# Hybrid pooling and mLSTM block: the values projected by rows of time, and the first keys made in place

## The chip, the cores and the metric

The kernel runs on one core of a Trainium2 chip. A core has a matrix engine (TensorE, PE), whose weight loads are listed apart (PEld), a vector engine (VectorE, DVE), a scalar engine (ScalarE, ACT), a general engine (GpSimd, POOL) and a queue engine for transfers (SyncE, SP). Each takes its own instructions in order and waits for the others by semaphores. The metric is the time of one execution on the device in microseconds (us). Lower is better.

## The reference

One block over 2048 steps of 1024 channels, batch 1, float32:

```python
h = rms_norm(x, norm_pre_g)
proj = h @ w_in                        # 1024 x 9232
u_a, z_a, q, k, v, o, z_b, gates, g_a, g_b = split(proj)
pooled = window means of u_a (2, 4, 8, 16) minus u_a
y_a = (pooled @ pool_mix_w, by group) * pool_scale * silu(z_a)
q, k = split(silu(centred_depthwise_conv([q, k], 5 taps)))
# 4 heads of 256; forward and backward, in chunks of 128 steps
c_chunk = einsum('bhcld,bhcle->bhcde', kw, vc)    # kw = weighted keys
C_t = keep * C_(t-1) + add * c_chunk
num = ((q k^T) * d) v + inter_scale * (q C);  h = num / max(|den|, exp(-m))
y_b = rms_norm(h_fwd + h_bwd) * mlstm_norm_g * sigmoid(o) * silu(z_b)
merged = sigmoid(g_a + b0) * (y_a @ w_proj_pool) + sigmoid(g_b + b1) * (y_b @ w_proj_mlstm)
out = x + rms_norm(merged @ w_out, norm_post_g)
```

## The kernel before

All products keep float32 accuracy by three matmuls on split operands: an upper part (made mostly on ACT, line 98) and a lower part, which is the rest (a subtraction on POOL or DVE, line 102). `mm3` does upper by upper, upper by lower and lower by upper for four tiles of 128 rows of the contraction, which are twelve matmuls into one bank (lines 110 to 112). In names, `...h` and `...l` are upper and lower.

**Phase 1, the projection (0 to 1492 us).** Time is cut into two halves of 1024 steps, each half into two blocks of 512. The columns of `w_in` are taken in 36 pairs of two blocks of 128 columns, in the order of `in_pairs()`. For each pair and half the product is done by Strassen's scheme in `strassen`: seven products of twelve matmuls of 512 columns, into the banks A, B and C (two buffers each) instead of eight. Weights stand still in the array, x moves, and the result has channels on the partitions and time along the row. The combinations of x (`S1` to `S4`, made in `combos`) are made once a half; those of the weights (`T1` to `T4`) are made in `prep_w` in the first half, kept in memory by `keep_w`, and read back in the second by `again_w`. The first two pairs, of which the weights arrive while x is still prepared, go through `quarters` (eight products, lines 500 to 502). Beside them run the matmuls of the gates (`gps`, copied out as `gsb` on line 671) and small products that fold the pooling weights (`fps`, line 373); all three take turns in two buffers named `tr`. `busy` matmuls at the very start only keep the array at work. The loop of `phase1` interleaves a pair with the rest of the one before it: A and the S2 product of the new pair, then A22 by T4 and S4 by B22 of the old, then the new pair's S1, S3 and A12 products. `FOLDS` and `ROWS` say behind which pair other work is given out.

The values are needed with time on the partitions. So `pair_v` collects the transposed result of one head as rows `raw` (line 685) and turns it by 32 transposes (128 x 128 each, `vtr`, line 744) a head and half, splits it again (`vnh` on ACT, `vnl` on DVE) and stores it.

**Phase 2, the mLSTM (1492 to about 1830 us).** For head 0 a first backward pass comes ahead: for each chunk of 128 steps the stored `kT` is turned back by two transposes (`kt`, line 1311), copied by ACT as `kn`, weighted and split into keys (`keys`), multiplied with the values into `cu` (lines 1040 to 1042, 2 x 3 matmuls of 258 columns), and added to the state `cb` on DVE (line 1256). Later heads do the same beside other work. For that first pass `keys` has a path of its own: ACT scales to float32 (`kw`, line 1267), DVE casts (line 1268) and POOL subtracts (line 1269), in tiles of the pool `w1`, of which there are eight. All other keys go through `weigh`: ACT scales straight to the upper part (line 1244), DVE makes the lower in one pass (line 1245), in two buffers (`KB = 2`).

**After it** (to 2342 us) come the two branch projections (`paps`, and `pb` with 256 columns to a matmul), the merge and the output projection.

The order on each engine is that in which the program is written, moved by priorities and by `issue_after`, which ties an instruction behind another.

Of the kernel before, what the change touches and what calls it, by code (L numbers as in the profile page):

```python
# [38 lines left out]
PRE = 12  # L39
FOLDS = (2, 5, 7, 9, 12, 14, 16, 18)  # L40
ROWS = (3, 4, 6, 7, 9)
# [10 lines left out]
def in_pairs():  # L52

    base = dict(u=0, z=1024, q=2048, k=3072, v=4096, o=5120, zb=6144, ga=7184, gb=8208)
    one = {}
    for h in range(NH):
        for kind in ("q", "k", "v", "u", "z", "ga", "gb"):
            c = base[kind] + h * DH
            one[kind, h] = (kind, h, c, c + P)
    for j in range(8):  # L60
# [21 lines left out]
class Kernel:  # L82
# [122 lines left out]

    def combos(self, H, j, a11, a12, a21, a22):

# [13 lines left out]
    def operands(self, half, H, hp, wc, pool, psum):  # L221
# [4 lines left out]
        room = {}  # L226
        for b, q, where in ((0, 0, "raw"), (0, 2, "acc"), (0, 1, "acc"), (0, 3, "acc"), (1, 0, "raw"), (1, 2, "raw"), (1, 1, wc), (1, 3, wc)):
# [20 lines left out]
        def sums():  # L248
# [8 lines left out]
            for i in range(4):  # L257
                nc.tensor.matmul(ps[:, i : i + 1], acc[:, i * P : (i + 1) * P], self.one_c, start=True, stop=True)
# [40 lines left out]
        for b in range(2):  # L299
# [22 lines left out]
            yield  # L322
        ends = [self.combos(H, j, X[j][0], X[4 + j][0], X[j][1], X[4 + j][1]) for j in range(4)]
        yield
# [186 lines left out]
    def phase1(self):  # L511
        tc, nc, a = self.tc, self.nc, self.a
        with ExitStack() as es:
# [25 lines left out]
            for half in range(2):  # L539
# [53 lines left out]
                for i in range(2, n):  # L593
# [25 lines left out]


                    this, self.read_banks = work(i, W), []
                    next(this)
# [35 lines left out]
    def gates(self, half, H, W, psum, pool):  # L658
        nc = self.nc
        for b in range(2):  # L660
# [9 lines left out]
            g = pool.tile([32, BLK], F32, tag="p", name=self.nm("gsb"))  # L670
            nc.scalar.activation(g, ps, AF.Copy)
            t0 = half * HALF + b * BLK
# [58 lines left out]

    def pair_v(self, half, kind, h, H, W, psum, pool):
        nc = self.nc
        t = yield from self.collect(H, W, psum, pool, HALF, 0)
        for b in range(2):
            hi, lo = (pool.tile([P, 4, DH + 2], F32R, tag="acc", name=self.nm(f"vn{p}")) for p in "hl")
            nc.vector.memset(hi[:, :, DH:].bitcast(F32), 1.0)
            nc.vector.memset(lo[:, :, DH:].bitcast(F32), 0.0)
            for c2 in range(2):
                ps = psum.tile([P, 2, DH], F32, tag="tr", name=self.nm("vtr"), bufs=2)  # L740
                for c in range(2):
                    for i in range(2):
                        tt = (b * 4 + c2 * 2 + c) * P
                        nc.tensor.transpose(ps[:, c, i * P : (i + 1) * P], t[i][:, tt : tt + P], self.ident)
                cc = slice(c2 * 2, c2 * 2 + 2)
                self.split(hi[:, cc, :DH], lo[:, cc, :DH], ps, "act", "dve")
            c0 = half * 8 + b * 4
            for p, o in (("h", hi), ("l", lo)):
                nc.sync.dma_start(self.sp[f"v{p}{h}"][:, c0 : c0 + 4, :], o.bitcast(F32))

# [471 lines left out]
    def mlstm(self, turns, ends):  # L1222
        nc, tc, sp, col = self.nc, self.tc, self.sp, self.cols
        E = DH + 2
        with ExitStack() as es:
# [16 lines left out]
            def weigh(out, k, w):  # L1242

                nc.scalar.activation(out[0], k, AF.Copy, scale=w)
                nc.vector.scalar_tensor_tensor(
                    out[1], k, w, out[0].bitcast(F32), op0=ALU.mult, op1=ALU.subtract
                )

            def update(new, kw, v, old, keep):
# [10 lines left out]
            def keys(h, c, d):  # L1260

                if d == 1 and h == 0:

                    kw = self.w1.tile([P, 2, 512], F32, tag="w", name=self.nm("kw"))[:, 0, :DH]
                    k = self.w1.tile([P, 2, 512], F32R, tag="w", name=self.nm("k"))
                    out = k[:, 0, :DH], k[:, 1, :DH]
                    up = nc.scalar.activation(kw, kn[h, c // 4][:, c % 4, :], AF.Copy, scale=col["w"][:, ix(d, h, c)])
                    nc.vector.tensor_copy(out[0], kw)
                    nc.gpsimd.tensor_tensor(out[1], kw, out[0].bitcast(F32), op=ALU.subtract)
                    if c == NC_ // 2:  # L1270

                        none = last.tile([P, 1], F32, tag="none", name="none", bufs=1)
                        with tc.issue_after(up.ins):
                            nc.scalar.activation(none, self.one_c, AF.Exp)
                    return out
# [387 lines left out]
    def tail(self):  # L1663

        tc = self.tc
        with ExitStack() as es:
            w1 = self.w1 = es.enter_context(tc.tile_pool(name="w1", bufs=8, side="right", reuse_waits="tile"))
            self.kv = es.enter_context(tc.tile_pool(name="kv", bufs=KV, reuse_waits="tile"))
# [46 lines left out]
def layouts(i):  # L1715
# [3 lines left out]
    wk = w_in.reshape(KT, P, -1).transpose(1, 0, 2)  # L1719
    pair = [np.stack([wk[:, :, c : c + P].reshape(P, 2, 4, P) for c in cc], axis=2) for _, _, *cc in in_pairs()]  # L1720
    x = np.asarray(i["x"])[0]
# [42 lines left out]
```

## Time and profile before

| | |
|---|---|
| runs | 2341.11, 2343.8, 2347.96 us; median 2343.8 |
| profiled execution | 2344.1 us, its span 2342.3 us |
| granted TensorE clock, mean | 0.993 |
| matmuls | 11545 |
| transfers | 564.43 MB, mean 241 GB/s |

The times of the profile are counted from the start of the span. A row of the time line gives start, duration, engine, line, operation, result and operands; in brackets is how long the engine was idle before, and what ended it. A matmul's duration overlaps that of the next.

### The profile page before, as it was taken

The numbers are of one execution on the slowest core, as the hardware profiler recorded it, in microseconds if no ns is written. First come the engines' busy times: TensorE is split into PE (matmuls) and PEld (weight loads), VectorE is DVE, ScalarE is ACT, GpSimd is POOL, SyncE is SP. The second block draws the span as 40 slices with busy tenths as digits, with TensorE's granted clock in tenths as the row PEclk, the third lists the DMA queues.
The fourth block names the chain that finished last, engine by engine and source line by source line (L and its number), as shares of the span: only waits on it lengthen the run. The fifth ranks groups of instructions, "written<-read, shape, count | busy, mean of one in ns | idle before, by whom it ended". The sixth has DMA issues, their size and how long they took to land. (4 is left out here: it accounts for less than half of the span.)

```text
span 2342.3 us, 32965 instructions
## 1 busy us (share of the span) xinstructions
PE 2285.9 (98%) x11545; PEld 1938.1 (83%) x11545; DVE 1412.6 (60%) x2379; ACT 885.8 (38%) x1796; POOL 1184.2 (51%) x917
## 2 busy tenths in 40 slices
PE   7899999999999999999999999899999999999998
PEld 5788888888888788888878788699998888999886
DVE  6665656768765555546656565388887453454365
ACT  5334333333343423323333233467766221111342
POOL 4755545666664533356564555245556341233574
PEclk9999999999999999999999999899999999999999
DMA  5567766766685366788888787767767696677863
GB/s 211 188 237 271 259 222 223 265 234 219 222 296 206 110 203 212 228 297 279 295 298 287 265 299 270 258 193 246 238 190 243 219 321 227 214 277 256 329 207 126
DMA packets 233270, 564.43 MB, mean 241 GB/s; under 512 B 23568, under 2 KB 70800, under 8 KB 233104
## 3 DMA queue, kind: packets, MB, share of 16 engines
q1 hardware_dynamic: 233104, 562.33, 69.7%
q8 instruction: 91, 1.49, 0.3%
q14 instruction: 75, 0.61, 0.1%
HBM read 340.46 MB, written 221.77 MB: 240 GB/s over the span
## 5 line engine op out<-in xcount | busy, mean ns | idle before, releaser
L102 POOL TENSOR_TENSOR wB<-wraw,wB 128x512 fp32r<-128x512 f32 x220 | 333.1, 1518 | 293.3 <-ACT wB L98 232.7
L98 ACT ACTIVATE wB<-wraw 128x512 fp32r<-128x512 f32 x224 | 139.3, 626 | 268.7 <-PE bankB L112 121.9
L102 POOL TENSOR_TENSOR wT<-wt,wT 128x512 fp32r<-128x512 f32 x102 | 148.5, 1459 | 128.2 <-ACT wT L98 105.5
L718 DVE SCALAR_TENSOR_TENSOR acc<-raw,conv_w,acc 128x1026 f32<-128x1026 f32 (+1 forms) x96 | 151.2, 1587 | 10.5 <-ACT acc L713 9.7
L1040 PE MATMUL pb<-oxs,w_proj_mlstm 128*128 128x256 f32 x512 | 143.9, 281 | 0.7 <-DVE sga L1206 0.4
L1042 PE MATMUL pb<-oxs,w_proj_mlstm 128*128 128x256 f32 x512 | 143.9, 281 | 0.0
L1041 PE MATMUL pb<-oxs,w_proj_mlstm 128*128 128x256 f32 x512 | 143.8, 281 | 0.0
L98 ACT ACTIVATE wT<-wt 128x512 fp32r<-128x512 f32 x136 | 85.3, 629 | 153.5 <-PE bankB L112 60.4
L1385 POOL TENSOR_TENSOR qs<-q,isc 128x256 f32<-128x256 f32 x120 | 90.0, 754 | 93.1 <-PE num L1401 59.9
L110 PE MATMUL bankB<-S3h,wT 128*128 128x512 f32 x272 | 106.2, 390 | 3.6 <-DVE u L469 3.6
L110 PE MATMUL bankB<-A22h,wT 128*128 128x512 f32 x272 | 106.1, 390 | 2.1 <-DVE u L474 2.1
L110 PE MATMUL bankA<-A12h,wB 128*128 128x512 f32 x272 | 108.0, 397 | 0.0
L110 PE MATMUL bankC<-S4h,wB 128*128 128x512 f32 x272 | 106.2, 391 | 1.2 <-DVE raw L685 1.2
L112 PE MATMUL bankA<-A11h,wB 128*128 128x512 f32 x272 | 106.0, 390 | 1.3 <-POOL wB L102 1.3
L1025 POOL TENSOR_TENSOR nm<-nm,mask 128x256 f32<-128x256 f32 x64 | 60.4, 955 | 91.4 <-DMA nm<-negM 74.2
L111 PE MATMUL bankB<-S2l,wT 128*128 128x512 f32 x272 | 106.5, 392 | 0.0
L110 PE MATMUL bankC<-S1h,wT 128*128 128x512 f32 x272 | 106.4, 391 | 0.0
L111 PE MATMUL bankC<-S4l,wB 128*128 128x512 f32 x272 | 106.4, 391 | 0.0
L112 PE MATMUL bankA<-A12h,wB 128*128 128x512 f32 x272 | 106.2, 391 | 0.0
L110 PE MATMUL bankA<-A11h,wB 128*128 128x512 f32 x272 | 106.2, 390 | 0.0
L111 PE MATMUL bankA<-A12l,wB 128*128 128x512 f32 x272 | 106.1, 390 | 0.0
L112 PE MATMUL bankC<-S4h,wB 128*128 128x512 f32 x272 | 106.1, 390 | 0.0
(417 smaller groups left out, 7097.3 us busy)
## 6 DMA issues: line engine op xcount, KB each, us to landing
wt<-wT SPq DMA_DIRECT2D x136, 512.0 KB, 4.4
wT<-wt SPq DMA_DIRECT2D x136, 512.0 KB, 6.0
wraw<-in_w_in SPq DMA_DIRECT2D x98, 512.0 KB, 5.2
vh<-vnh SPq DMA_DIRECT2D x16, 516.0 KB, 4.4
vl<-vnl SPq DMA_DIRECT2D x16, 516.0 KB, 5.7
v<-vh SPq DMA_DIRECT2D x16, 516.0 KB, 8.8
v<-vl SPq DMA_DIRECT2D x16, 516.0 KB, 8.5
xT<-in_xT SPq DMA_DIRECT2D x16, 512.0 KB, 6.5
```

The costliest lines, as they stand in the source:

```text
L98: self.upper = nc.scalar.activation(hi, x, AF.Copy)
L102: return eng.tensor_tensor(lo, x, hi.bitcast(F32), op=ALU.subtract)
L110: nc.tensor.matmul(ps, wh, xh, start=start and kt == 0, stop=False, skip_group_check=True)
L111: nc.tensor.matmul(ps, wh, xl, start=False, stop=False, skip_group_check=True)
L112: end = nc.tensor.matmul(ps, wl, xh, start=False, stop=stop and kt == 3, skip_group_check=True)
L718: nc.vector.scalar_tensor_tensor(acc[:, :n], raw[:, tap : tap + n], self.cw[:, ct, tap : tap + 1], acc[:, :n], op0=ALU.mult, op1=ALU.add,)
L1025: nc.gpsimd.tensor_tensor(t[:, d, :, :], t[:, d, :, :], mask[:, d, None, :].to_broadcast([P, 2, P]), op=ALU.add)
L1040: nc.tensor.matmul(ps, wh, xh, start=i == 0, stop=False)
L1041: nc.tensor.matmul(ps, wh, xl, start=False, stop=False)
L1042: nc.tensor.matmul(ps, wl, xh, start=False, stop=i == n)
L1385: nc.gpsimd.tensor_tensor(qs[d], q[:, :, ck], isc[:, d, j % 2, None, :].to_broadcast([P, 2, P]), op=ALU.mult)
```

## The change

1. **Values.** The weights of four v pairs are now cut otherwise: pairs `v0` and `v1` hold the 2 x 256 columns of heads 0 and 1, each for one half of the contraction; `v2` and `v3` the same for heads 2 and 3. `by_rows` multiplies with x standing (128 steps of time) and 256 columns of weights moving, so that the result has time on the partitions: seven Strassen products of 48 matmuls a group and half, each filling both buffers of a bank (four tiles of 128 x 256). The matmuls of a product are tied behind its first. `pair_v` adds and splits straight out of the banks. The transposes and `raw` are gone. The group runs when its second pair's weights are there, with nothing interleaved.
2. **Order of the projection.** `in_pairs` is written out anew: both v groups come early (after q0 and q1), and o, z and the gates fill in otherwise. One number of `FOLDS` is 10 instead of 9.
3. **First blocks.** In the first half the lower part of `S1` is made on DVE instead of POOL. Two room assignments of x are swapped. The first `busy` stands behind the `ssqp` matmuls, and the second is doubled. The preparation of the fourth pair's weights is tied behind `gsb` and a copy out of the first banks.
4. **First pass's keys.** All keys go through `weigh`, in their own buffers; the path by `w1`, the casts and POOL's subtractions are gone.

```diff
-FOLDS = (2, 5, 7, 9, 12, 14, 16, 18)
+FOLDS = (2, 5, 7, 10, 12, 14, 16, 18)
...
-        self.put(H, "S1", j, s1, "act", "pool")
+        self.put(H, "S1", j, s1, "act", le)          # "dve" in half 0, "pool" in half 1
...
-            busy(X[7][0][:, :P], X[7][0])
+            with tc.issue_after(done.ins):           # done: last ssqp matmul
+                busy(X[7][0][:, :P], X[7][0])
...
-            busy(self.rstd[:, :1].to_broadcast([P, P]), X[7][0])
+            for _ in range(2):
+                busy(self.rstd[:, :1].to_broadcast([P, P]), X[7][0])
...
-                            with tc.issue_after(self.scaled[8].ins) if i == 2 else ExitStack():
+                            ties = [self.scaled[8]] if i == 2 else [self.evac, self.gated] if i == 3 else []
...
+                    if self.pairs[i][0] == "v":
+                        if self.pairs[i][1][1] == 0:
+                            first = W
+                            run(rest)
+                        else:
+                            run(work(i, (first, W)))
+                        rest = iter(())
...
+    def by_rows(self, H, W, psum, pool, out):
+        bank = {(k, s): psum.tile([P, 2, DH], ...) for k in "ABC" for s in range(2)}
+        def prod(k, h, w, start):
+            for t in range(2):
+                wh, wl = (x.rearrange("p (k a) n -> p k (a n)", k=2) for x in W[t][w])
+                for tt in range(4):
+                    ps = bank[k, tt // 2][:, tt % 2, :]
+                    for j in range(2):
+                        hh, hl = (x[:, 2 * t + j, tt * P : (tt + 1) * P] for x in H[h])
+                        # hh by wh, hh by wl, hl by wh
...
+        prod("A", "A11", "B11", True);  p1 = copy("A")
+        prod("B", "S2", "T2", True);    u2 = plus("B", p1)
+        prod("C", "S1", "T1", True)
+        prod("B", "S3", "T3", False);   u3 = plus("B", p1)
+        give(3, "C", u3)
+        prod("A", "A12", "B21", False); give(0, "A", None)
+        prod("B", "A22", "T4", False);  give(2, "B", p1)
+        prod("C", "S4", "B22", False);  give(1, "C", u2)
...
     def pair_v(...):
-                        nc.tensor.transpose(ps[:, c, i * P : (i + 1) * P], t[i][:, tt : tt + P], self.ident)
-                self.split(hi[:, cc, :DH], lo[:, cc, :DH], ps, "act", "dve")
+            lower = self.split(
+                hi[:, cc, :DH], lo[:, cc, :DH], x.rearrange("p (c n) -> p c n", c=2), "act", "dve"
+            )
...
     def keys(h, c, d):
-                if d == 1 and h == 0:
-                    up = nc.scalar.activation(kw, kn[h, c // 4][:, c % 4, :], AF.Copy, scale=...)
-                    nc.vector.tensor_copy(out[0], kw)
-                    nc.gpsimd.tensor_tensor(out[1], kw, out[0].bitcast(F32), op=ALU.subtract)
                 out = split2(io, [P, DH], f"k{d}", bufs=KB)
-                weigh(out, kn[h, c // 4][:, c % 4, :], col["w"][:, ix(d, h, c)])
+                up = weigh(out, kn[h, c // 4][:, c % 4, :], col["w"][:, ix(d, h, c)])
```

Three places show how instructions moved; the numbers behind a name tell tiles apart. The first is POOL while x and the first weights are prepared: `S1l` and `S3l` are lower parts of x (four blocks of channels each), `fm` is of the folds, `wB` is that of the third pair's weights. Before:

```order
L366 TENSOR_TENSOR fm_818<-fm_818 128x512
L102 TENSOR_TENSOR S1l_413<-xT_312,S1h_412 128x512
L102 TENSOR_TENSOR S1l_413<-xT_314,S1h_412 128x512
L102 TENSOR_TENSOR S1l_413<-xT_312,S1h_412 128x512
L102 TENSOR_TENSOR S1l_413<-xT_314,S1h_412 128x512
L102 TENSOR_TENSOR S3l_415<-xT_311,S3h_414 128x512
L102 TENSOR_TENSOR S3l_415<-xT_313,S3h_414 128x512
L102 TENSOR_TENSOR S3l_415<-xT_311,S3h_414 128x512
L102 TENSOR_TENSOR S3l_415<-xT_313,S3h_414 128x512
L102 TENSOR_TENSOR wB_85_827<-wraw_823,wB_85_827 128x512
```
After:

```order
L373 TENSOR_TENSOR fm_820<-fm_820 128x512
L105 TENSOR_TENSOR S3l_417<-xT_311,S3h_416 128x512
L105 TENSOR_TENSOR S3l_417<-xT_312,S3h_416 128x512
L105 TENSOR_TENSOR S3l_417<-xT_311,S3h_416 128x512
L105 TENSOR_TENSOR S3l_417<-xT_312,S3h_416 128x512
L105 TENSOR_TENSOR wB_86_829<-wraw_825,wB_86_829 128x512
```
POOL's four `S1l` are gone from ahead of `S3l` (they stand on DVE), and the weights follow earlier.

The second is ACT, some ten instructions later: `sg` empties the banks of the first two pairs, `gsb` the gates', `wB_110` and `wT_113` (after: `wB_111`, `wT_114`) are upper parts of the fourth pair's weights. Before:

```order
L841 ACTIVATE sg_781<-bankC_636,b_merge 128x512
L98 ACTIVATE wB_110_956<-wraw_952 128x512
L841 ACTIVATE sg_784<-bankC_637,b_merge 128x512
L98 ACTIVATE wT_113_963<-wt_961 128x512
L841 ACTIVATE sg_793<-bankA_644,b_merge 128x512
L98 ACTIVATE wT_114_966<-wt_959 128x512
L841 ACTIVATE sg_796<-bankB_645,b_merge 128x512
L671 ACTIVATE gsb_801<-gps_688 32x512
L98 ACTIVATE wT_116_971<-wt_969 128x512
```
After:

```order
L930 ACTIVATE sg_783<-bankC_638,b_merge 128x512
L930 ACTIVATE sg_786<-bankC_639,b_merge 128x512
L930 ACTIVATE sg_795<-bankA_646,b_merge 128x512
L930 ACTIVATE sg_798<-bankB_647,b_merge 128x512
L692 ACTIVATE gsb_803<-gps_690 32x512
L101 ACTIVATE wB_111_958<-wraw_954 128x512
L101 ACTIVATE wT_114_965<-wt_963 128x512
L101 ACTIVATE wT_115_968<-wt_961 128x512
L101 ACTIVATE wT_117_973<-wt_971 128x512
```
The fourth pair's weights, which stood between the four `sg` and ahead of `gsb`, stand behind them.

The third is PE at the start of the first backward pass: `kt` are transposes, `cu` the sums of head 0. Before:

```order
L1311 MATMUL kt_12039<-ident,kT_11903 128x128 x2
L1311 MATMUL kt_12059<-ident,kT_11903 128x128 x2
L1311 MATMUL kt_12082<-ident,kT_11992 128x128 x2
L1311 MATMUL kt_12106<-ident,kT_11992 128x128 x2
L1311 MATMUL kt_12126<-ident,kT_11992 128x128 x2
L1311 MATMUL kt_12146<-ident,kT_11992 128x128 x2
L1311 MATMUL kt_12164<-ident,kT_12079 128x128 x2
L1040 MATMUL cu_11853<-v_1720_11825,k_11839 128x258
L1041 MATMUL cu_11853<-v_1721_11826,k_11839 128x258
L1040 MATMUL cu_11858<-v_1720_11825,k_11839 128x258
L1041 MATMUL cu_11858<-v_1721_11826,k_11839 128x258
L1040 MATMUL cu_11873<-v_1720_11825,k_11848 128x258
```
After:

```order
L1392 MATMUL kt_12324<-ident,kT_12311 128x128 x2
L1392 MATMUL kt_12332<-ident,kT_12311 128x128 x2
L1392 MATMUL kt_12351<-ident,kT_12311 128x128 x2
L1392 MATMUL kt_12370<-ident,kT_12311 128x128 x2
L1129 MATMUL cu_12341<-v_1673_12315,k_1679_12328 128x258
L1130 MATMUL cu_12341<-v_1674_12316,k_1679_12328 128x258
L1129 MATMUL cu_12346<-v_1673_12315,k_1679_12328 128x258
L1130 MATMUL cu_12346<-v_1674_12316,k_1679_12328 128x258
L1129 MATMUL cu_12360<-v_1673_12315,k_1682_12336 128x258
L1130 MATMUL cu_12360<-v_1674_12316,k_1682_12336 128x258
L1131 MATMUL cu_12341<-v_1673_12315,k_1680_12329 128x258
L1131 MATMUL cu_12346<-v_1673_12315,k_1680_12329 128x258
```
Before, all sixteen pairs of transposes of head 0 (and one of the next) come ahead of the first sum; now the sums begin after four, and transposes and sums alternate.

More of the change, by code (lines that the diff above doesn't have):

```diff
@@ L226, in operands @@
         room = {}
[L227 removed]
+        for b, q, where in ((0, 0, "raw"), (0, 2, "acc"), (0, 1, "acc"), (0, 3, "acc"), (1, 0, "raw"), (1, 1, "raw"), (1, 2, wc), (1, 3, wc)):
             if where is wc:
@@ L322, in operands @@
             yield
-        ends = [self.combos(H, j, X[j][0], X[4 + j][0], X[j][1], X[4 + j][1]) for j in range(4)]
+        ends = [self.combos(H, j, X[j][0], X[4 + j][0], X[j][1], X[4 + j][1], ("dve", "pool")[half]) for j in range(4)]
         yield
@@ L618, in phase1 @@
                         self.keep_w(W, i)
+                    if self.pairs[i][0] == "v":
[5 more added lines that the diff above has]
+                        rest = iter(())
+                        if half == 0 and i + 1 in FOLDS:
+                            next(fold)
+                        continue
                     this, self.read_banks = work(i, W), []
@@ L730, in late_load, with copy, plus, give @@
         return kind, h, raw
-    def pair_v(self, half, kind, h, H, W, psum, pool):
+    def by_rows(self, H, W, psum, pool, out):
         nc = self.nc
[L734 to L745, printed above, removed]
-                self.split(hi[:, cc, :DH], lo[:, cc, :DH], ps, "act", "dve")
-            c0 = half * 8 + b * 4
-            for p, o in (("h", hi), ("l", lo)):
-                nc.sync.dma_start(self.sp[f"v{p}{h}"][:, c0 : c0 + 4, :], o.bitcast(F32))
+        bank = {
+            (k, s): psum.tile([P, 2, DH], F32, tag=f"bank{k}", name=self.nm(f"bank{k}"), bufs=2)
+            for k in "ABC" for s in range(2)
+        }
+        flat = lambda x: x.rearrange("p c n -> p (c n)")
+        def prod(k, h, w, start):
[5 more added lines that the diff above has]
+                        hh, hl = (x[:, 2 * t + j, tt * P : (tt + 1) * P] for x in H[h])
+                        opens, end = start and t + j + tt % 2 == 0, t + j == 2
+                        with self.tc.issue_after(opened.ins) if start and not opens else ExitStack():
+                            one = nc.tensor.matmul(ps, hh, wh[:, j], start=opens, stop=False, skip_group_check=True)
+                        if opens:
+                            opened = one
+                        nc.tensor.matmul(ps, hh, wl[:, j], start=False, stop=False, skip_group_check=True)
+                        self.third = nc.tensor.matmul(ps, hl, wh[:, j], start=False, stop=end, skip_group_check=True)
+        def copy(k):
+            o = [pool.tile([P, BLK], F32, tag="p", name=self.nm("p1")) for _ in range(2)]
+            for s in range(2):
+                nc.scalar.activation(o[s], flat(bank[k, s]), AF.Copy)
+            return o
+        def plus(k, add):
+            o = [pool.tile([P, BLK], F32, tag="p", name=self.nm("u")) for _ in range(2)]
+            for s in range(2):
+                nc.vector.tensor_tensor(o[s], flat(bank[k, s]), add[s], op=ALU.add)
+            return o
+        def give(i, k, add):
+            for s in range(2):
+                out(i, s, flat(bank[k, s]), add and add[s])
+        prod("A", "A11", "B11", True)
+        p1 = copy("A")
+        prod("B", "S2", "T2", True)
+        u2 = plus("B", p1)
+        yield
+        prod("C", "S1", "T1", True)
+        prod("B", "S3", "T3", False)
+        u3 = plus("B", p1)
+        yield
+        give(3, "C", u3)
+        prod("A", "A12", "B21", False)
+        give(0, "A", None)
+        yield
+        prod("B", "A22", "T4", False)
+        give(2, "B", p1)
+        prod("C", "S4", "B22", False)
+        give(1, "C", u2)
+        yield
@@ new lines, in pair_v, with out @@
+    def pair_v(self, half, kind, at, H, W, psum, pool):
+        nc = self.nc
+        made = {}
+        def out(i, s, ps, add):
+            x = ps
+            if add is not None:
+                x = add
+                nc.vector.tensor_tensor(x, ps, add, op=ALU.add)
+            if s == 0:
+                made[i] = tuple(pool.tile([P, 4, DH + 2], F32R, tag="acc", name=self.nm(f"vn{p}")) for p in "hl")
+            hi, lo = made[i]
+            cc = slice(2 * s, 2 * s + 2)
+            lower = self.split(
+                hi[:, cc, :DH], lo[:, cc, :DH], x.rearrange("p (c n) -> p c n", c=2), "act", "dve"
+            )
+            if s == 1:
+                with self.tc.issue_after(lower.ins):
+                    nc.vector.memset(hi[:, :, DH:].bitcast(F32), 1.0)
+                    nc.vector.memset(lo[:, :, DH:].bitcast(F32), 0.0)
+                h, c0 = at[0] + 2 * (i % 2), half * 8 + i // 2 * 4
+                for p, o in (("h", hi), ("l", lo)):
+                    nc.sync.dma_start(self.sp[f"v{p}{h}"][:, c0 : c0 + 4, :], o.bitcast(F32))
+        yield from self.by_rows(H, W, psum, pool, out)
@@ L1719, in layouts, with columns @@
     wk = w_in.reshape(KT, P, -1).transpose(1, 0, 2)
-    pair = [np.stack([wk[:, :, c : c + P].reshape(P, 2, 4, P) for c in cc], axis=2) for _, _, *cc in in_pairs()]
+    def columns(kind, at, *cc):
+        if kind != "v":
+            return np.stack([wk[:, :, c : c + P].reshape(P, 2, 4, P) for c in cc], axis=2)
+        rows = wk.reshape(P, 2, 2, 2, -1)[:, :, at[1]]
+        return np.stack([rows[..., c : c + DH] for c in cc], axis=2).reshape(P, 2, 2, 4, P)
+    pair = [columns(*p) for p in in_pairs()]
     x = np.asarray(i["x"])[0]
```

44 lines of the change are left out of this document (23 added, 21 removed).

## The prediction

> **What bounds the kernel now.** I read the page's engine table first, then the weight of single matmuls in the time line, then TensorE's waits, then stretches in which it is not full. In the table the columns are busy time, share of the span and instructions:
>
> ```profile
> span 2342.3 us, 32965 instructions
> PE 2285.9 (98%) x11545; PEld 1938.1 (83%) x11545; DVE 1412.6 (60%) x2379; ACT 885.8 (38%) x1796; POOL 1184.2 (51%) x917
> ```
>
> TensorE (PE) is busy 98%, the next engine 60%. So time is gained only by fewer or shorter PE streams, by PE's waits, or by its clock. What a stream costs is the distance between starts, since a matmul's own duration overlaps the next. Twelve matmuls of 512 columns (one Strassen product) stand between these two rows of PE's time line (start, duration):
>
> ```profile
> 1480.24 0.39 PE L110 MATMUL bankC<-S1h,wT 128*128 128x512 f32 x1
> ...
> 1482.96 0.39 PE L110 MATMUL bankB<-S3h,wT 128*128 128x512 f32 x1
> ```
>
> 2.72/12 = 0.227 us each. The nearest rows for 256 columns with a fresh stationary tile for each are those of the second projection (durations min/median/max, first and last start):
>
> ```profile
> L1042 PEld LDWEIGHTS pb<-oxs,w_proj_mlstm x512: 187/188/194, 1994.0 to 2176.4; 128*128 128x128 f32 x171
> ...
> L1040 PE MATMUL pb<-oxs,w_proj_mlstm x512: 275/281/385, 1993.8 to 2176.3; 128*128 128x256 f32 x171
> ...
> L1042 PE MATMUL pb<-oxs,w_proj_mlstm x512: 274/281/297, 1994.1 to 2176.5; 128*128 128x256 f32 x171
> ```
>
> 3 x 512 matmuls in 2176.5 - 1993.8 = 182.7 us: 0.119 us each, although each has a weight load of 0.188. The loads lie under other streams. PE's waits (us, times, longest), of which these rows bear on the change:
>
> ```profile
> PE fps L373 <- ACT gsb L671: 5.6, 1, 5.6
> PE vtr L744 <- DVE raw L685: 5.0, 3, 3.9
> PE kt L1311 <- DMA kT<-kT: 4.2, 3, 2.3
> PE bankB L110 <- DVE u L469: 3.6, 3, 1.7
> PE bankB L110 <- DVE u L474: 2.9, 3, 1.3
> PE cu L1040 <- DVE k L1268: 1.8, 1, 1.8
> PE bankA L112 <- POOL wB L102: 1.3, 1, 1.3
> ```
>
> Stretches (first column the window, second its length; the granted clock is the third figure from the end):
>
> ```profile
> core 0: us, PE busy (x) PEld busy (x) DVE busy (x) ACT busy (x) POOL busy (x), PEclk, DMA share, GB/s
> 70.00:95.00 25.00, 18.09 (x70) 13.90 (x69) 18.17 (x15) 12.79 (x25) 20.99 (x14) 0.86 0.62 216
> 1230.00:1233.30 3.30, 3.17 (x11) 2.88 (x12) 2.75 (x5) 1.20 (x2) 0.00 (x0) 0.51 0.98 209
> 1235.00:1480.00 245.00, 243.26 (x1077) 201.19 (x1076) 140.18 (x156) 77.19 (x117) 127.43 (x84) 1.00 0.77 267
> 1492.00:1510.00 18.00, 10.19 (x44) 6.63 (x43) 3.62 (x7) 10.08 (x26) 1.45 (x2) 0.61 1.04 408
> 1510.00:1530.00 20.00, 17.17 (x109) 15.79 (x109) 16.55 (x46) 12.01 (x30) 13.95 (x19) 0.84 0.87 301
> 1496.00:1516.00 20.00, 12.91 (x51) 10.03 (x52) 7.11 (x16) 13.42 (x34) 6.62 (x10) 0.50 0.94 356
> ```
>
> The projection is full (243.26 of 245), except at 70 to 95 us and round 1230. The hand-over to the first backward pass at 1492 is the emptiest place: PE works 10.19 of 18 us, at clock 0.61.
>
> **The change part by part.**
>
> 1. *Values.* Removed are 128 transposes:
>
> ```profile
> L744 PE MATMUL vtr<-ident,raw 128*128 128x128 f32 x128 | 18.0, 282 | 5.0 <-DVE raw L685 5.0
> ...
> 1492.23 0.60 PE L1311 MATMUL kt<-ident,kT 128*128 128x128 f32 x4
> ```
>
> The second row, from the time line, gives the distance of such transposes: (0.60 - 0.28)/3 = 0.107 us. So 128 x 0.107 = 13.7 us go, with their waits of 5.0. The longest wait (3.9) stands just ahead of the half-clock stretch at 1230, in which 3.17 us were worked at 0.51; I count 0.8 of the lost 1.6, since other late adds could still empty PE there. Against it, 4 pairs x 2 halves x 7 x 12 = 672 matmuls of 512 become 2 groups x 2 halves x 7 x 48 = 1344 of 256: 1344 x 0.119 - 672 x 0.227 = 159.9 - 152.5 = +7.4. Sum: -13.7 - 5.0 - 0.8 + 7.4 = **-12.1**. On the other engines little moves: per two pairs VectorE (DVE) has 18 passes of 512 columns before and after (adds and lower parts), ScalarE (ACT) 12 and then 10; the stores keep count and size. Each group's halves of the weights are another cut of the same columns, loaded by as many transfers.
>
> The Trainium skill, page "TensorE: Matmul & The Clock Gate", section "Back-to-back issue gap", speaks against this edit: spacing is set by load and stream together, about 81 ns at 128 columns and 131 at 512. Read in between, about 98 ns at 256 (an estimate from that page), it would give 1344 x 0.098 - 672 x 0.131 = +44 us. The rows above (227 and 119 ns) disagree with it in this kernel, and the sum goes by the rows.
>
> 2. *New waits of the values.* by_rows holds both buffers of all three banks. Each bank is read (copy, add, split) while a product of 48 x 0.119 = 5.7 us runs in another, and one such read is two DVE passes of 0.61 (the S2l row below, 1.84/3), so inside a group there is cover; if DVE is late the price is a wait. What is not covered is the entry: the first product fills both buffers of bank A, and the second is the one that the pair before has just filled; PE reaches it 12 x 0.119 = 1.4 us later, and behind PE's wait everything is queued. The longest such wait among the bank rows is 1.7, so 4 groups give at most 6.8. The reordered list brings also the late convolutions of the second half closer together, on a DVE that already keeps bankB waiting (3.6 and 2.9). Above, I bound it by all 28 product borders at a DVE pass with its hand-over, 0.7, = 20; below by -6, if the new order happens to end the bankB waits. I take **+2.5**, near the entry's row, as the list shows three waits in 1400 us.
>
> 3. *The stage at 70 to 95.* These rows of the time lines of GpSimd (POOL), ACT, DVE and PE belong together; the bracket is the idle time before, and its releaser:
>
> ```profile
> 54.32 14.99 POOL L102 TENSOR_TENSOR S1l<-xT,S1h 128x512 fp32r<-128x512 f32 x4 [3.71 <-ACT S1h L98]
> 69.27 5.95 POOL L102 TENSOR_TENSOR S3l<-xT,S3h 128x512 fp32r<-128x512 f32 x4
> 69.34 0.63 ACT L98 ACTIVATE wB<-wraw 128x512 fp32r<-128x512 f32 x1 [9.07 <-POOL S1l L102]
> 70.53 1.84 DVE L102 TENSOR_TENSOR S2l<-xT,S2h 128x512 fp32r<-128x512 f32 x1 [6.11 <-ACT S2h L98]
> 76.50 0.50 PE L112 MATMUL bankA<-A11h,wB 128*128 128x512 f32 x1 [1.34 <-POOL wB L102]
> 86.29 0.63 ACT L98 ACTIVATE wT<-wt 128x512 fp32r<-128x512 f32 x1 [1.79 <-DVE wt L426]
> 88.48 0.57 ACT L671 ACTIVATE gsb<-gps 32x512 f32<-32x512 f32 x1
> 81.64 1.89 PE L373 MATMUL fps<-fm,fw 128*128 128x256 f32 x8
> 89.11 3.35 PE L373 MATMUL fps<-fm,fw 128*128 128x256 f32 x7 [5.57 <-ACT gsb L671]
> ```
>
> POOL takes 3.75 us for each S1l, and ACT and DVE stand behind it. PE loses 1.3 at wB and 5.57 at fps, whose bank waits for gsb, which ACT reaches only at 88.48 behind the uppers of pair 3; the 7 matmuls after it take 3.35 at half clock where 8 took 1.89, which costs 1.7. The window loses 25 - 18.09 = 6.9 to idle; with that and some products after fps still at half clock it is about 9. The change moves the four S1l to DVE (4 x 0.61 = 2.4 us, where DVE had 6.11 idle), so POOL reaches S3l about 15 us earlier, and ties pair 3's preparation behind gsb, so ACT's row is four sg, gsb. The banks are full before 76; between 86.29 and 88.48 ACT did four instructions, 0.55 each, so 4 x 0.55 + 0.57 more puts gsb near 79, and PE wants it at 81.64. Behind the tie stand the upper, and so the POOL lower, of wB for the first value product. PE gets to it 38 matmuls of 512 after fps's row, 8.6 us, enough for an upper (0.63) and a lower (1.5). I take **-9**; it could be -6 if half a window at half clock stays, and 6.9 + 25 x (1 - 0.86) = 10.4 is all there is to gain. Without the cover, wB late by one POOL pass costs 1.5.
>
> 4. *The start.* PE runs the first products at half clock:
>
> ```profile
> 17.24 1.91 PE L281 MATMUL busy<-xT,rstd 128*128 128x512 f32 x2
> 20.43 0.79 PE L500 MATMUL bankA<-A11h,wB 128*128 128x512 f32 x1 [1.27 <-ACT A11h L98]
> ...
> 24.86 0.43 PE L502 MATMUL bankA<-A11l,wB 128*128 128x512 f32 x1
> ```
>
> Ten matmuls from 20.43 to 24.86 take 0.44 each instead of 0.23. Twice the filler from 17.24 fills the 1.27 gap and lets the clock rise some 3 us earlier; it ends 0.2 after A11h is ready. 3 x 0.48 - 0.2 = **-1.2**, between 0 and -1.6.
>
> 5. *First backward pass.* Between 1492 and 1530 PE is idle 7.81 + 2.83 = 10.6, and from 1496 to 1516 half of 12.91 busy is lost to the clock: 17.1 us in all.
>
> ```profile
> 1501.22 2.25 PE L1311 MATMUL kt<-ident,kT 128*128 128x128 f32 x8 [1.62 <-DMA kT<-kT]
> 1505.78 0.66 PE L1311 MATMUL kt<-ident,kT 128*128 128x128 f32 x2 [2.30 <-DMA kT<-kT]
> 1508.23 0.58 PE L1040 MATMUL cu<-v,k 128*128 128x258 f32 x1 [1.79 <-DVE k L1268]
> 1504.53 0.88 DVE L1245 SCALAR_TENSOR_TENSOR k<-kn,col_w,k 128x256 fp32r<-128x256 f32 x2 [11.41 <-ACT k L1244]
> 1527.06 4.47 DVE L1256 SCALAR_TENSOR_TENSOR cb<-cb,col_keep,cu 128x258 f32<-128x258 f32 x11
> ```
>
> All transposes of head 0 come first and wait for each arriving kT; the sums (cu) begin at 1508.23, with the casts behind two rows of L1245 that waited for ACT 11.41 us. Changed, transposes and sums alternate from about 1494.5, and the keys take ACT and DVE, as the L1245 rows do, without POOL. DVE then sets the pace: 18 lowers x 0.44 + 28 updates x 0.41 = 19.4 us, against 34 x 0.107 + 90 x 0.12 (258 columns, near pb's 256) = 14.4 on PE. So it ends near 1492.2 + 2.3 + 19.4 = 1514, later than the last kT (1505.6), and PE has lost about 7 there: gain 17.1 - 7 = 10. With two key buffers a chunk passes ACT (an upper part, taken like DVE's lower), DVE behind two updates, PE (6 x 0.12), and four hand-overs of 0.1: (0.44 + 0.82 + 0.44 + 0.72 + 0.4)/2 = 1.4 us, 16 x 1.4 + 2.3 = 25 and a gain of only 17.1 - (25 - 14.4) = 6.5; one window at half clock takes 1.7 more. Ends -3 and -12; I take **-9**, nearer DVE's own pace.
>
> The same page's Part 1 says that an idle window of about 3.4 us sets the clock to half and a busy one sets it back. The stretch at 1230 agrees (3.30 us at 0.51 behind a wait of 3.9); by that rule an alternating stream that leaves no such gap stays at full clock, as the -9 has it.
>
> **Sum:** -12.1 + 2.5 - 9 - 1.2 - 9 = -28.8. The profiled run took 2344.1 (span 2342.3; the median of the runs is 2343.8, 0.3 below): 2344.1 - 28.8 = **2315 us**.
>
> **Rivals.**
> (a) *The first pass keeps its length.* DMA share is 1.04 there, and kT arrives as before; if the two buffers or arrivals set the pace and the clock stays at half, term 5 falls away: 2324. For it: the waits for kT. Against: they end at 1505.6, the sums only at 1526.
> (b) *DVE falls behind in the value groups*, so PE waits at most borders: +20 instead of +2.5 gives 2333. For it: bankB waits for DVE already; against: 60% busy and 5.7 us of cover. With (a) too it would be 2342, no change.
> (c) *Slower: loads no longer hide.* If the 672 additional loads stood between streams, 672 x 0.188 = +126 would replace the +7.4: 2434. If only the load's length bounded the pace, 1344 x 0.188 - 152.5 = +100: 2408. It decides from a pace of 0.119 + 28.8/1344 = 0.140 us on. Against: 1536 pb matmuls at 0.119 with equal loads. The page's Part 3, under "What overlaps and what doesn't", has loads overlap only where row groups differ; by that rule this rival would come, and the pb rows do not bear it out.
>
> **How the numbers follow.** A measurement tells about 0.3% (7 us) from no change. Forecast 0.62, (a) alone 0.17, (b) alone 0.13, (a) with (b) 0.03, (c) 0.05. Low end: terms at their good ends, -12.9 - 6 - 10.4 - 1.6 - 12 = -43, all at once unlikely; I put 0.07 below 2303. High end: (b) at 2334, which leaves (c), both together and a part of (b), about 0.13. Faster 0.62 + 0.17 + 0.10 = 0.89; same 0.03 + 0.03 = 0.06; slower 0.05. For the forecast alone 2307 to 2322.
>
> **What would show it.** By steps: (1) by_rows' starts 0.119 apart, no vtr; 0.14 or more is (c). (2) PE's waits at banks A to C: under 7 us in all; near 20 is (b). (3) no wait of fps, window 70 to 95 at clock 1.0. (4) starts 0.23 apart before 22 us. (5) first cu before 1500 less the time gained earlier, clock near 1.0; a half-clock stretch of 15 us or more is (a). It would be wrong if a new wait of over 5 us stood at a place that I call covered, above all wB of the first value group or a convolution ahead of an add.

## The result, and the profile after

The changed kernel takes 2328.1 us (median of 5 runs, 2326.5 to 2329.4), against 2345.1 in the runs beside it: a ratio of 0.9926, 95% interval 0.9912 to 0.9939, or 17 us less. The forecast was 2315, with a range of 2303 to 2334. The sign and the range held; the forecast gain was 29 us and 17 came of it. The profiled run took 2327.45. The top of its page, then PE's waits and the stretches that answer to those of before (same columns):

```profile
span 2325.7 us, 34053 instructions
PE 2280.1 (98%) x12091; PEld 1958.7 (84%) x12091; DVE 1436.8 (62%) x2383; ACT 882.5 (38%) x1788; POOL 1165.3 (50%) x898
```

```profile
PE bankB L113 <- DVE u L476: 10.5, 4, 5.5
PE bankB L113 <- DVE u L481: 7.4, 6, 4.5
...
PE kt L1392 <- ACT kn L1395: 1.6, 2, 1.4
```

```profile
70.00:95.00 25.00, 19.53 (x78) 15.65 (x77) 16.32 (x14) 8.83 (x18) 17.32 (x12) 0.86 0.83 295
...
1235.00:1480.00 245.00, 238.56 (x1033) 196.42 (x1032) 127.01 (x139) 71.72 (x109) 119.57 (x81) 0.98 0.74 253
1489.00:1515.00 26.00, 23.55 (x157) 19.85 (x156) 21.35 (x52) 19.59 (x51) 3.61 (x5) 1.00 0.94 349
```

The waits of fps, of vtr and for the transfers of kT are gone. In their place PE waits 17.9 us in bank B for DVE's adds (6.5 before). The clock at 70 to 95 us is 0.86 as before, and the end of the projection, which was full, has lost 5 us. Only the first backward pass is as hoped: 157 matmuls in 26 us at clock 1.00. The same stretch of before, up to the first num that reads the state (num<-cb, 1531.24; after, 1514.69):

```profile
1492.00:1531.00 39.00, 28.36 (x158) 23.42 (x157) 21.17 (x54) 22.09 (x55) 15.40 (x21) 0.74 0.93 344
```

By milestones in both time lines:

- up to the gates' last matmul of the first half, 1.9 us less (74.29, now 72.36);
- from there to the second half's first gates, 6.3 less (693.1, 686.8);
- from the second half's last gates to the first kt, 5.0 more (670.7, 675.7);
- from the first kt to the last num, 13.8 less (338.1, 324.3);
- after that, 0.4 more.

### The profile page after: what moved, and what is told of

Same layout as the page of the kernel before. It is cut to its first block, busy times and chain, and to the rows that moved or that the text cites. A ratio compares the mean times of both kernels' runs of the same rounds, so it can differ in the third digit from the quotient of the medians.

```text
span 2325.7 us, 34053 instructions
## 1 busy us (share of the span) xinstructions
PE 2280.1 (98%) x12091; PEld 1958.7 (84%) x12091; DVE 1436.8 (62%) x2383; ACT 882.5 (38%) x1788; POOL 1165.3 (50%) x898
## 5 line engine op out<-in xcount | busy, mean ns | idle before, releaser
L105 POOL TENSOR_TENSOR wB<-wraw,wB 128x512 fp32r<-128x512 f32 x220 | 332.5, 1516 | 333.4 <-ACT wB L101 271.1
L739 DVE SCALAR_TENSOR_TENSOR acc<-raw,conv_w,acc 128x1026 f32<-128x1026 f32 (+1 forms) x96 | 154.8, 1627 | 13.3 <-ACT acc L734 12.4
L113 PE MATMUL bankB<-S3h,wT 128*128 128x512 f32 x240 | 96.6, 402 | 10.7 <-DVE u L476 10.5
L113 PE MATMUL bankB<-A22h,wT 128*128 128x512 f32 x240 | 95.1, 396 | 6.6 <-DVE u L481 6.3
L433 DVE TENSOR_TENSOR wt<-wraw,wt 128x512 f32<-128x512 f32 x68 | 62.9, 926 | 62.4 <-POOL wT L105 46.5
L1129 PE MATMUL paps<-pys,w_proj_pool 128*128 128x512 f32 x256 | 101.0, 395 | 0.0
L1130 PE MATMUL paps<-xa,w_proj_pool 128*128 128x512 f32 x256 | 100.8, 394 | 0.1
L1131 PE MATMUL paps<-pys,w_proj_pool 128*128 128x512 f32 x256 | 100.7, 394 | 0.0
L476 DVE TENSOR_TENSOR u<-bankB,p 128x512 f32<-128x512 f32 x68 | 46.6, 686 | 84.8 <-PE bankB L115 84.0
L1615 POOL TENSOR_TENSOR pa<-pa,sgb 128x256 f32<-128x256 f32 x64 | 48.1, 769 | 99.9 <-DVE sgb L1614 65.4
L1129 PEld LDWEIGHTS pb<-oxs,w_proj_mlstm 128*128 128x128 f32 x512 | 96.5, 188 | 0.3 <-DVE sga L1295 0.3
L1131 PEld LDWEIGHTS pb<-oxs,w_proj_mlstm 128*128 128x128 f32 x512 | 96.7, 189 | 0.0
L1130 PEld LDWEIGHTS pb<-oxs,w_proj_mlstm 128*128 128x128 f32 x512 | 96.4, 188 | 0.0
L115 PE MATMUL bankB<-S3h,wT 128*128 128x512 f32 x240 | 95.6, 398 | 0.0
```

The lines of the kernel that those rows point to most:

```text
L105: return eng.tensor_tensor(lo, x, hi.bitcast(F32), op=ALU.subtract)
L113: nc.tensor.matmul(ps, wh, xh, start=start and kt == 0, stop=False, skip_group_check=True)
L115: end = nc.tensor.matmul(ps, wl, xh, start=False, stop=stop and kt == 3, skip_group_check=True)
L433: nc.vector.tensor_tensor(t, x, y, op=ALU.subtract)
L739: nc.vector.scalar_tensor_tensor(acc[:, :n], raw[:, tap : tap + n], self.cw[:, ct, tap : tap + 1], acc[:, :n], op0=ALU.mult, op1=ALU.add,)
L1129: nc.tensor.matmul(ps, wh, xh, start=i == 0, stop=False)
```

## The experiments

**Each part alone.** The kernel before, with one part of the change each. The edits are the diff's own lines. First the keys, part 4 of the diff (`keys` and `weigh`).

> The kernel before, with the change of the first pass's keys alone (ACT and DVE make them in their own two buffers; no casts, no subtraction on POOL). Theory A, from the two traces: the first backward pass alone gives most of the gain, because its half-clock stretch of 20 us goes with its waits; 13 to 14 us less than before, and no half-clock stretch after the projection. Theory B, the size in the prediction: 9 us less, DVE's pace or the two buffers holding it. Rival (a): nothing, under 3 us. If part of the gain needed the projection's new order, it would come out under 9.

Measured: 2327.5 us, ratio 0.9936 (0.9922 to 0.995), 15 us less; the window 1489 to 1516 is at clock 1.00. Theory A. The keys alone are nearly the whole result.

The start, part 3 of the diff: `le`, the rooms, `busy` and the tie `ties = ... [self.evac, self.gated] if i == 3`.

> The kernel before, with the change of the first blocks alone (lower part of S1 on DVE, rooms swapped, busy matmuls, the fourth pair's weights tied behind gsb). Theory A: the wait of fps goes, and a wait of the S3 product for DVE's first add (u, L469) takes its place, as in the changed kernel; about 2 us at the start and 1 in the stage, 3 us less than before, and the half-clock stretch near 88 us stays. Theory B, the prediction's terms 3 and 4: 10 us less, and no half-clock stretch before 100 us.

Measured: 2341.5, ratio 0.9993 (0.9985 to 1.0002): 1.6 us less, which cannot be told from nothing. PE's waits have the new entry, and the window 70 to 95 stays at clock 0.86:

```profile
PE bankB L110 <- DVE u L473: 7.6, 3, 5.4
```

```profile
70.00:95.00 25.00, 19.56 (x79) 15.68 (x78) 17.07 (x16) 9.57 (x19) 16.74 (x12) 0.86 0.87 303
```

Theory A. The values with the order of the projection, parts 1 and 2:

> The kernel before, with the change of the values and of the order of the projection alone (parts 1 and 2). Theory A, from the traces: some 5 us gained in the first half and as many lost in the second, where bank reads on DVE come late; within 3 us of before. Theory B, the prediction's terms 1 and 2: 9 to 10 us less than before.

Measured: 2342.7, ratio 0.9996 (0.9985 to 1.0006): nothing that can be told (1 us less by the ratio, 1 more by the medians). In its trace the first half's stretch is 4.2 us shorter and the second's 5.6 longer; its waits:

```profile
PE bankB L113 <- DVE u L472: 8.9, 7, 2.0
PE bankB L113 <- DVE u L477: 8.0, 5, 5.1
```

Theory A again. The parts alone add to 15 + 1.6 + 0.9 = 17.5, the whole gave 17; each part is known to 2 or 3 us.

**Where the keys' gain comes from.** The kernel before with the short path, but in the old tiles:

```diff
+                if d == 1 and h == 0:
+                    k = self.w1.tile([P, 2, 512], F32R, tag="w", name=self.nm("k"))
+                    out = k[:, 0, :DH], k[:, 1, :DH]
+                else:
+                    out = split2(io, [P, DH], f"k{d}", bufs=KB)
                 up = weigh(...)
```

> The kernel before, with the first pass's keys made by ACT and DVE alone (no casts, nothing on POOL), but still in the tiles of w1. It tells whether the gain of the keys comes from the engines or from the place. Theory P (place): the tiles of w1 come free only when what stood there in the projection is done, so all transposes still stand ahead of the first sum and the half-clock stretch stays; within 4 us of before. Theory E (engines): the shorter path gives most of it, 10 us or more less than before, as the keys in their own places gave 15.

Measured: 2341.8, ratio 0.9993 (0.9982 to 1.0004). Theory P: the short path alone gains nothing, and against the keys alone only the tiles differ. From the time lines of PE and ACT in this kernel:

```profile
1502.73 0.66 PE L1307 MATMUL kt<-ident,kT 128*128 128x128 f32 x2 [2.40 <-DMA kT<-kT]
1504.80 0.58 PE L1040 MATMUL cu<-v,k 128*128 128x258 f32 x1 [1.41 <-ACT k L1244]
...
1500.85 0.91 ACT L1244 ACTIVATE k<-kn,col_w 128x256 fp32r<-128x256 f32 x2
1503.43 0.38 ACT L1310 ACTIVATE kn<-kt 128x256 f32<-128x256 f32 x1 [1.68 <-PE kt L1307]
1503.85 2.51 ACT L1244 ACTIVATE k<-kn,col_w 128x256 fp32r<-128x256 f32 x6
```

All transposes, the next head's among them, still come first, and ACT makes keys only from 1500.85 on. No cast and no POOL pass is left on the path, and nothing is gained. The long path in tiles of its own was not run, so the place is shown to be needed, not to be enough.

**The wait at 84 us.** The changed kernel, one tie more:

```diff
-  ties = ... [self.evac, self.gated] if i == 3 else []
+  ties = ... [self.evac, self.gated, self.read_banks[0]] if i == 3 else []
```

> The changed kernel, with the fourth pair's weights tied also behind the third pair's first add (u, L476), so that DVE makes the add ahead of the five weight differences. Theory A (the add is late only because those stand ahead of it): the wait of 5.5 us at 84 us and the half-clock stretch behind it go, 6 to 8 us less than the changed kernel, near 2321. Rival: the weights are then late in turn, a new wait of the first value group takes its place, and the time stays within 2 us of the changed kernel's 2328.

The rows it rests on, of the changed kernel's DVE, ACT and PE:

```profile
83.19 0.68 DVE L433 TENSOR_TENSOR wt<-wraw,wraw 128x512 f32<-128x512 f32 x1
83.97 0.69 DVE L105 TENSOR_TENSOR wT<-wt,wT 128x512 fp32r<-128x512 f32 x1
85.84 1.74 DVE L433 TENSOR_TENSOR wt<-wraw,wt 128x512 f32<-128x512 f32 x1 [1.17 <-POOL wT L105]
87.61 1.64 DVE L433 TENSOR_TENSOR wt<-wraw 128x512 f32<-128x512 f32 x1
89.18 0.68 DVE L476 TENSOR_TENSOR u<-bankB,p 128x512 f32<-128x512 f32 x1
...
78.66 0.57 ACT L692 ACTIVATE gsb<-gps 32x512 f32<-32x512 f32 x1
83.31 1.67 ACT L101 ACTIVATE wT<-wt 128x512 fp32r<-128x512 f32 x3 [3.55 <-DVE wt L433]
84.88 0.58 ACT L470 ACTIVATE p<-bankA 128x512 f32<-128x512 f32 x1
...
89.91 0.80 PE L113 MATMUL bankB<-S3h,wT 128*128 128x512 f32 x1 [5.47 <-DVE u L476]
```

gsb is there at 78.66, as forecast (near 79). But p, which the add needs, stands on ACT behind three uppers of the next pair, and the add on DVE behind that pair's differences. With the tie the add comes at 81.78 and the window is at full clock:

```profile
81.78 0.68 DVE L476 TENSOR_TENSOR u<-bankB,p 128x512 f32<-128x512 f32 x1
82.38 0.68 DVE L433 TENSOR_TENSOR wt<-wraw 128x512 f32<-128x512 f32 x1
```

```profile
70.00:95.00 25.00, 23.42 (x111) 19.42 (x110) 18.37 (x18) 10.58 (x21) 18.03 (x13) 1.00 0.83 298
```

Measured: 2322.0 (2320.4 to 2324.9), ratio 0.9910 (0.9896 to 0.9923) to before, where the changed kernel had 0.9926. That is 6 us by the medians and 4 by the ratios, whose intervals overlap; the runs do not, and the trace is 7 us shorter. Theory A; a wait of 1.6 us comes up at 91 us.

**The late adds of the second half.** Rows of the changed kernel's ACT, DVE and PE at the longest:

```profile
1243.48 0.63 ACT L101 ACTIVATE wp<-wp 128x512 fp32r<-128x512 f32 x1 [12.71 <-DMA wT<-wt]
...
1244.14 0.69 DVE L105 TENSOR_TENSOR wp<-wp,wp 128x512 fp32r<-128x512 f32 x1 [9.67 <-ACT wp L101]
1244.75 0.69 DVE L706 TENSOR_TENSOR raw<-bankC,u 128x512 f32<-128x512 f32 x1
1245.35 3.02 DVE L864 TENSOR_TENSOR win<-win 128x1036 f32<-128x1036 f32 x2
1248.40 2.83 DVE L868 SCALAR_TENSOR_TENSOR pooled<-win,raw 128x1032 f32<-128x1032 f32 x1
...
1251.96 0.68 DVE L481 TENSOR_TENSOR u<-bankB,p 128x512 f32<-128x512 f32 x1
...
1252.69 0.79 PE L113 MATMUL bankB<-A22h,wT 128*128 128x512 f32 x1 [4.47 <-DVE u L481]
```

DVE stands 9.67 us idle at wp's lower part, with a read of bank C, the pooling windows and the add behind it. wp shares three tiles with the masks (nm). In every third turn there are two masks, and wp's upper part gets the tile of the first of them, whose store was issued in that turn. The row above names another transfer, which landed at 1242.5; the mask's store landed at 1243.25, and wp's upper ran at 1243.48. Over the kernel (ACT's waits; before the change 16.3, 4, 4.8):

```profile
ACT wp L101 <- DMA nm<-nm: 36.1, 5, 9.6
```

The edit takes wp first:

```diff
+                    if half == 1 and PRE <= i < PRE + 2 * KT:
+                        with tc.issue_after(self.read.ins):
+                            self.split_ahead(*divmod(i - PRE, KT))
                     if half == 1:
                         with tc.issue_after(self.read.ins):
...
                                 self.masked(u, mask)
-                    if half == 1 and PRE <= i < PRE + 2 * KT:
-                        with tc.issue_after(self.read.ins):
-                            self.split_ahead(*divmod(i - PRE, KT))
```

> The changed kernel, with the pieces of w_proj_pool (wp) taken ahead of the masks (nm) in each turn of the second half, so that wp's buffer is no longer one whose mask was stored in the same turn. Theory A: of the new waits for DVE in the second half those at 1194 and 1248 us come from wp's lower part, which DVE must do first and which waits for that store; they go with their half-clock stretches, 6 to 10 us less than the changed kernel, near 2320. Rival: DVE's other work there (pooling windows, convolutions) makes the add late anyway, and the time stays within 3 us of 2328.

Measured: 2322.4 (2322.0 to 2323.0), ratio 0.9909 (0.9896 to 0.9922), trace 5 us shorter; ACT no longer waits for a mask's store, and the longest late add of this half is 2.5 us. By the medians that is just under theory A's 6 us, by the ratios 4. Its account holds only in part. PE's waits for the adds are not less in all: 12.2 us in the second half, 12.4 without the edit. What is less is the half clock behind them, 3.4 us of it instead of 13.7, which is worth 5. So the gain of this edit is in the clock behind the waits, not in the waits.

The next two move other work instead:

```diff
- elif half == 1 and waits is None and late and i >= 10:
+ elif half == 1 and waits is None and late and i in (11, 14, 16, 22, 24, 27, 29, 32):
```

> The changed kernel, with the late convolutions of the second half given out at the turns at which they stood before (13, 15, 18, 23, 26, 28, 31, 33 instead of 11, 13, 15, 18, 21, 23, 26, 28). Theory C: the new order brings the convolutions closer together, and that makes DVE late; 6 to 12 us less than the changed kernel, and PE's waits for DVE in the second half under 6 us. Theory A (wp behind the masks' store is the cause, not the convolutions): within 3 us of 2328, the waits near 1194 and 1248 us as before.

Measured: 2320.6 (2319.8 to 2324.7), ratio 0.9903 (0.9887 to 0.9919). Time as theory C has it by the medians (7 us), but its waits are between: ACT still waits 39.6 us for masks, the wait at 1248 is gone, and four of 1.1 to 2.7 us remain in the second half, where theory C had under 6 us in all.

The other moves the second value group in `in_pairs` from q1 to k2, and each o a place forward:

```diff
-    light = [[("v", 0), ("v", 1)], [("o", 0)], [("v", 2), ("v", 3)], [("o", 1)], [("o", 2)], [("o", 3), ("z", 0)]]
+    light = [[("v", 0), ("v", 1)], [("o", 0)], [("o", 1)], [("o", 2)], [("o", 3)], [("o", 4), ("z", 0)]]
...
+    light += [[("o", 5), ("z", 1)], [("v", 2), ("v", 3)], [("o", 6), ("z", 2)], ...
```

> The changed kernel, with the second group of values at turns 20 and 21 instead of 8 and 9 (the convolutions then come at 12, 14, 17, 23 and later). Theory D: a value group is slack for DVE (its bank reads have 5.7 us of cover), and having both groups before turn 10 leaves a run of pairs without slack; 6 to 12 us less than the changed kernel. Rival: the group's own 18 passes on DVE then meet convolutions, windows and wp, and the time is the same or longer than 2328.

Measured: 2323.4 (2322.6 to 2324.9), ratio 0.9912 (0.9897 to 0.9927). Better than the changed kernel by 5 us by the medians and 3 by the ratios, less than theory D's 6. The late adds are shorter (14.2 us in all, 17.9 without), but the group itself now waits 4.5 us for its weights. Theory D is not separated from C by this, since the convolutions move too.

**Together.** Edits one and two of the above (add first, wp ahead), then with the convolutions' turns as a third, and that with S1 on POOL again:

```diff
-  ("dve", "pool")[half]
+  "pool"
```

> The changed kernel with both edits, the fourth pair's weights behind the third pair's first add, and wp ahead of the masks. Theory A: the two causes are apart, the gains add, 11 to 13 us less than the changed kernel, near 2316. Rival: each loosens only what the next wait takes up, and the two together give no more than one, near 2321.

> The changed kernel with all three edits: the fourth pair's weights behind the first add, wp ahead of the masks, the convolutions at their turns of before. Theory A with C (masks' store and crowded convolutions are two causes of the late adds): 3 to 5 us less than with the first two edits, near 2313, and PE's waits for DVE in the second half under 6 us. Rival: the convolutions mattered only through the same late wp, and the time stays within 2 us of 2317.

> As the kernel with all three edits, but with the lower part of S1 on POOL again in the first half (as before the change). Theory A: POOL is slow there only while DVE works beside it, as S3l took 4 us each on POOL in the changed kernel; the move to DVE took 5 us off POOL's chain, of which PE saw the wait for wB (1.3 us) and some of the lateness of S2 and S4, so 2 to 4 us more than with the three edits. Theory B, the prediction's: without the move POOL is 15 us later, and 5 us or more are lost. Rival: no difference, under 1 us.

Measured: two edits 2316.9, ratio 0.9883 (0.9869 to 0.9898); three 2316.3, 0.9886 (0.9868 to 0.9903); with S1 on POOL 2317.2, 0.9890 (0.9872 to 0.9907). The first two add (theory A), to 10 us under the changed kernel by the ratios. The third edit adds nothing, which was the rival: it seems to have worked on the same waits. S1's engine makes no difference that can be told, as the rival has it: theory A's 2 us would lie within the noise, theory B's 5 do not show. POOL's rows with S1 there again, and of the changed kernel without it:

```profile
52.27 14.40 POOL L105 TENSOR_TENSOR S1l<-xT,S1h 128x512 fp32r<-128x512 f32 x4 [3.70 <-ACT S1h L101]
66.62 6.42 POOL L105 TENSOR_TENSOR S3l<-xT,S3h 128x512 fp32r<-128x512 f32 x4
```

```profile
54.95 16.05 POOL L105 TENSOR_TENSOR S3l<-xT,S3h 128x512 fp32r<-128x512 f32 x4 [6.26 <-ACT S3h L101]
70.96 1.28 POOL L105 TENSOR_TENSOR wB<-wraw,wB 128x512 fp32r<-128x512 f32 x1
```

Whatever four passes POOL has first there take some 15 us, and most of that is the first pass. In order, the four of the kernel before, of the changed kernel, and with S1 on POOL again (durations in ns, min/median/max, then first and last start):

```profile
L102 POOL TENSOR_TENSOR S1l<-xT,S1h x4: 1282/1287/11244, 54.3 to 68.0; 128x512 fp32r<-128x512 f32 x4
L105 POOL TENSOR_TENSOR S3l<-xT,S3h x4: 1282/1286/12298, 54.9 to 69.7; 128x512 fp32r<-128x512 f32 x4
L105 POOL TENSOR_TENSOR S1l<-xT,S1h x4: 1282/1294/10643, 52.3 to 65.4; 128x512 fp32r<-128x512 f32 x4
```

The first pass ends only when DVE has ended its run of passes. In the changed kernel that is here:

```profile
65.42 0.68 DVE L105 TENSOR_TENSOR S2l<-xT,S2h 128x512 fp32r<-128x512 f32 x1
73.53 1.76 DVE L433 TENSOR_TENSOR wt<-wraw,wt 128x512 f32<-128x512 f32 x1 [7.43 <-POOL wT L105]
```

Some 10 us of waits for the adds of line 481 are left in all three; what would take them away was not tried.

## Why the prediction was right and wrong

- **Keys (-9): right in mechanism, too small.** Alone they gave -15 (-18 to -12), and -13.3 from the first kt to the first num<-cb in the two traces. DVE sets the pace as forecast: lower and two updates every 1.18 us.

```profile
1498.02 0.48 DVE L1334 SCALAR_TENSOR_TENSOR k<-kn,col_w,k 128x256 fp32r<-128x256 f32 x1
1498.42 0.87 DVE L1346 SCALAR_TENSOR_TENSOR cb<-cb,col_keep,cu 128x258 f32<-128x258 f32 x2
1499.20 0.48 DVE L1334 SCALAR_TENSOR_TENSOR k<-kn,col_w,k 128x256 fp32r<-128x256 f32 x1
```

  At 0.12 us each, 158 matmuls are some 19 us of work, so before lost 39 - 19 = 20 and the changed kernel 26 - 19 = 7. The 7 was in the forecast. The 20 was taken as 17.1, because idle time and half-clock time were summed, and a busy PE between spaced matmuls hides the rest. The shade of 1 for two key buffers was not needed: DVE's rows show few gaps. Rival (a) is out, kT's arrivals no longer hold PE. That the short path was enough, as the part on POOL and casts suggests, is refuted by the old tiles' run.
- **Start (-1.2):** full clock came earlier as said, from 20.9 us instead of 24.9, and the trace has -1.9, beyond the -1.6 given as the end. That the edit did it is not shown. The run with the values alone has the start of before, and there the first products are at full clock from 20.57 and the first half's gates end at 72.0.
- **Stage (-9): the step that failed**, with about 1 us gained (1.3 in the trace of the start alone, from the first half's last gates to the second's first). Its first half held (gsb near 79, no wait of fps, no wait for wB). But of the work behind the tie only wB was costed, which the value group needs later. The add for S3's bank is needed before that, and it stands behind the same pair's work on ACT and DVE. The wait moved from fps to that bank, from 84.4 instead of 83.5 us on, and with it the half clock. Nor was POOL what its row seemed to say. S1l's 14.99 us were not four passes of 3.75, but one of 11.24, which lasted until DVE's run had ended, and three of 1.3. Without S1l, POOL did reach S3l 14.3 us earlier (54.95), but then S3l's first pass stood for 12.3 us, and POOL was done with S3l only 4 us earlier (71.0, before 75.2). DVE's price of 0.61 a pass was right by luck: the row it was read from (S2l, 1.84) is one pass, not three, and such a slow one came twice ahead of the late add (1.74 and 1.64, in the rows of the wait at 84 us).
- **Values (-12.1) and their waits (+2.5): the second was the mis-sized one.** The pace is as forecast. Of the first product of 48, 37 matmuls stand between the starts of these rows, 0.120 apart:

```profile
104.47 0.28 PE L777 MATMUL bankA<-wB,A11l 128*128 128x256 f32 x1
...
108.90 0.28 PE L773 MATMUL bankB<-wT,S2h 128*128 128x256 f32 x1
```

  So 1344 x 0.120 - 152.5 = +8.8, and the 128 transposes (16 a head and half, not the 32 of the kernel's description) are gone with their waits; the weight loads are hidden and rival (c) is out. The Trainium skill's page "TensorE: Matmul & The Clock Gate", section "Back-to-back issue gap", gives about 81 ns at 128 columns and 131 at 512; the estimate of 98 read between them does not hold here: 120 ns. But the second half lost 5 us where it should have gained 6: new waits and half-clock stretches of some 11 us. That goes towards rival (b) in size, not in place. The value groups' own products wait 0.1 us in all. At the entry feared most, PE did 11 matmuls of the first product (from 97.69), then 24 of the pair before (from 99.00), then these 37. The pairs after the groups do wait, on adds behind wp, pooling windows and convolutions. The forecast looked for the price at by_rows' own borders.
- **Sum:** -15 for -9, -1.6 for -10.2, -0.9 for -9.6. That the time lies in the range is in part luck: the keys' 6 us too many stand against 17 that did not come.

## What to carry to other kernels

When a tie or a reordering takes a wait away, list what each in-order engine then does between that wait and the next thing the bound engine needs; the next wait stood 12 matmuls further, behind the work that had been moved. Work on the bound engine that looks like pure cost (transposes) may be the slack in which a slower engine catches up; no run here separates that from the new order of the other work. And a small tile shared by two kinds of work can put a store's landing into a chain of adds, as the masks did.

## What the runs showed of the hardware

A pass with two inputs on POOL and a run of such passes on DVE did not share the time. The first S3l pass of the changed kernel took 12.30 us, from 54.95 on, beside DVE passes that start 0.60 apart until 66.10; the next three took 1.28 each. DVE was not slowed there. Where single passes of both alternate, both take longer: round 87 us POOL's take 1.72 and DVE's 1.64 to 1.74, instead of 1.28 and 0.68. The Trainium skill's page "SBUF — State Buffer", section "Who interferes with whom", says that a DVE instruction with two inputs in SBUF and a GpSimd one that reads SBUF exclude each other for a whole instruction, and that the order of issue decides who is held. The trace agrees with the exclusion: one pass of 1.28 us lasted 12.30. It fits that the choice of engine for S1 was worth nothing.

What a short wait of PE costs is not told by its length. In the changed kernel those of 1.9 us at 1194 and 2.0 at 1321 were each followed by 3.4 us at half clock, and that of 4.5 at 1248 by 6.8; one of 2.8 us at 1301 with the three edits was followed by none. The same wait of 5.4 us at 84 us was followed by 6.8 us with the convolutions at their turns of before (clock 0.79 from 84 to 100) and by 3.4 with wp first (0.89), though neither edit touches that place. So a difference of 1.7 us between two single traces can be this alone.
